# Two ends of an up-projection: a half sum and a copy moved, a whole product ahead of a wait, a bank copied out, and three scan bursts tied

## The chip, the cores and the metric

One core of a Trainium2 chip runs the whole program. The metric is the device time of one execution in microseconds (us), taken as the median of several runs.

## The reference, cut to what matters

The reference is one layer of a diffusion backbone with 128 prompt tokens and 1024 latent tokens (a 16 x 64 grid), model width 1024, all in fp32.

```python
h = rmsnorm(x, norm1) * (1 + scale1) + shift1
mix, new_gla, new_hgrn = hybrid_mixer(h, ...)     # two gated linear scans, forward and backward, then @ w_out
x = x + gate1 * mix
h = rmsnorm(x, norm2) * (1 + scale2) + shift2
u = dw_conv(h @ w_up, conv_w, conv_b, grid)       # 3x3 on the grid; width 3 over the prompt
gate, up = jnp.split(u, 2, axis=-1)               # FFN_HIDDEN = 2816 each
x = x + gate2 * ((jax.nn.silu(gate) * up) @ w_down)
y = rmsnorm(x, final_norm)
```

The scans run in eight heads of two kinds. The change touches the last of the scans and the line `u = dw_conv(h @ w_up ...)`; everything else is as it was.

## The kernel before, in words

**Numbers.** Each fp32 operand of a large product is split into a high half (a rounded fp32r copy, made by ACT) and a low half (the rest, made by DVE or POOL on line 69). PE then computes high x high, high x low and low x high. So a weight tile costs one ACT instruction, one DVE or POOL instruction and three products.

**Order.** A framework places the instructions of each engine: in a simulated schedule it takes, for each engine, what is ready by its model of costs and of priority. `tc.issue_after(ins)` adds an order: what is issued under it comes behind `ins` on its engine. `run(eng, fn)` chains the steps of the first hidden group this way. What carries no such tie can come out in another order than in the text. The names in `anchor` hold the instructions to which later ones are tied.

**Scan stage** (to about 600 us). The loop runs over six head groups `n`, in each over three thirds (`bi`, with block `b` from `ORDER = (2, 1, 0)`), in each over eight slots with two parts. In slots 0, 2, 4 and 6 `levels` issues a burst of small PE products (L964) under high priority. Between the bursts `stream(goal, ...)` issues the fill: products of projections and of w_out that the bursts don't depend on (L625, L639, L777), as far as `GOALS` say for this slot. `anchor["fill"]` is the last fill product and `anchor["paced"]` is the one behind which the next burst is tied. For `n < 5` that tie is set anew in every even slot. The last group, `n == 5`, pops it at its start, so its bursts have none; its fill is the gate weights' L625, evacuated by ACT on L676.

**Up stage** (about 780 to 1270 us). The loop runs over 22 hidden groups `c` of 128 gate and 128 up channels. The product of a group's weights with the 1024 latent tokens is done in seven half-size products instead of eight, as Strassen's method does: `up(c, p)` with p from 1 to 7, each 12 PE instructions of 512 columns (`up_product`, L1777). Their operands are token sums (`b11`, `b21`, `b22`, `t1` to `t4`, made once) and weight sums (`s1` to `s4`, made for each group). They collect in PSUM in two tiles of a group, `F, S = u[c]`; there are three such tiles in all. In between, ACT copies three partial results to SBUF (`copy`, L1971: product 1 to `p1`, product 6 to `u2`, product 5 to `p5`) and DVE adds them: `p1` and `u2` to the halves of F (L2134 and L2135; L1869 and L1870 for the first group), `p5` to S (L2160). Then `conv_rows` forms the 3x3 convolution: ACT's first tap (L1931) and eight DVE steps (L1943) for each half of the channels. `second_gate` applies silu (ACT, L2043), multiplies gate by up on POOL (L2045) and stores it from POOL's queue.

The prompt's product (`up_prompt`, L2009) goes into a bank of its own; it is copied to SBUF and turned by two PE transposes (`prompt_columns`) into a bank `pp` from the same pool `ps_p`. `conv_prompt` reads `pp` with an ACT tap (L1956) and two DVE steps (L1960) for gate and up, four DVE steps in a group.

Weights of the next groups are split with POOL's help: `split_slots` issues ACT's high half (L1759) and POOL's low half (L69); `weight_sums` are POOL's too, and the loads of a row that waits for its tile (`load_row`) stand in SP's queue.

At `c == 21`, the last group, product 3 is issued in two: its first two of four row blocks (`range(2)`, six PE instructions), then the third `u` tile is taken and product 1 issued, then the other six. The third tile comes free when the convolution that reads it has ended.

**Down stage** (from about 1270 us). Seven products (`product`, L2279, L2333), each over eleven pairs of hidden groups, with four row tiles; in the first one the first three pairs go together (`head=3`). `load_w` loads a pair, ACT splits its high half (L133), and the low half (L69) is POOL's for the first pairs and DVE's from then on. The PSUM banks of this stage lie where those of the up stage lay.

Of the kernel before, what the change touches and what calls it, by code (L numbers as in the profile page):

```python
# [12 lines left out]
AF = mybir.ActivationFunctionType  # L13
ALU = mybir.AluOpType
# [3 lines left out]
P = 128  # L18
# [6 lines left out]
NHID = 22  # L25
# [24 lines left out]
def kernel(ctx: ExitStack, tc: tile.TileContext, ins, outs, stop=None):  # L50
    nc = tc.nc
# [10 lines left out]
    anchor = {}  # L62
# [339 lines left out]
    for i in range(2):  # L402
# [3 lines left out]
        for v in range(2):  # L406
            dst = bass.AP(t.tensor, t.offset + v * pitch, [[32 * pitch, 2], [1, 512]])
# [4 lines left out]
    for i in range(2):  # L412
        ps = (ps_a, ps_mm)[i].tile([2 * 32, 512], F32, name="ada", tag=("ada", "mm")[i])
        psA.append(ps)
        for kt in range(KT):
# [4 lines left out]
            for j in range(2):  # L420
# [4 lines left out]
                    start=(kt == 0),  # L425
                    stop=(kt == KT - 1),
# [754 lines left out]
    def ada_load(spare=False):  # L1181
        if ada_todo:
            g, kt, half = ada_todo.pop(0)
            if spare:
                piece = flat(vp.tile([P, NTILE, P], F32, name="v", tag="v"))[:, 0:1024]
                piece = piece.rearrange("p (j n) -> p j n", j=4)
            else:
                piece = rawp.tile([P, 4, 256], F32, name="raw", tag="raw")
            n0 = "ABC".index(g) * 2048
            src = w_ada[kt * P : (kt + 1) * P, n0 : n0 + 2048].rearrange("p (j h n) -> p h j n", j=4, h=2)  # L1190
            nc.sync.dma_start(piece, src[:, half])
            ada_open.append((g, kt, half, piece))
# [41 lines left out]
    for n, u in enumerate(groups):  # L1234
        if not u.gla:
            u.v = [u.vpair[u.hd % 2]]
        if n == 0:
            start_group(u)
            ready = gates(u, 2)
        if n == 5:  # L1240
            anchor.pop("paced")
        for bi, b in enumerate(ORDER):
            fb, k, k0 = ready
            lv = levels(u, b, fb, k, k0)
            for slot in range(8):
                at = 8 * bi + slot
                last = anchor["mm"] = next(lv)
                if (2, 0, 6) <= (n, bi, slot) < (5, 0, 0) and slot % 2 == 0:
                    with tc.issue_after(last.ins):
                        with tc.high_priority(offset=BURST_AHEAD):  # L1250
                            ada_product()
                        ada_load(spare=(n, bi) >= (2, 2))
                with tc.issue_after(last.ins):
                    outs_.step("half", at)
                    states.step("product")
                if slot == 5 and (b > 0 or n < 5):
                    if b > 0:
                        ready = gates(u, b - 1)
                    else:
                        start_group(groups[n + 1])  # L1260
                        ready = gates(groups[n + 1], 2)
                for part in range(2):
                    with tc.issue_after(last.ins):
                        if part == 0:
                            states.step("keys")
                            if n == 5:
                                while slots["held"]:
                                    slots["held"].pop(0)()
                        outs_.step("full", at)
                        if part == 1:  # L1270
                            outs_.step("full", at)
                    goal = GOALS[n] + (GOALS[n + 1] - GOALS[n]) * (16 * bi + 2 * slot + part + 1) / 48
                    stream(goal, None if n == bi == 0 else anchor["mm"] if n == 5 else last)
                    if n < 5 and slot % 2 == 0 and part == 1:
                        anchor["paced"] = anchor["fill"]
            drain(lv)
            states.drain()
            states = Steps(state_steps(u, b, k))
        outs_.drain()
        outs_ = Steps(out_steps(u))  # L1280
# [13 lines left out]
    def run(eng, fn):  # L1294

        if ran.get("free"):
            return fn()
        with tc.issue_after(ran[eng].ins) if eng in ran else nullcontext():
            ran[eng] = fn()
# [103 lines left out]
    tt = nc.vector.tensor_tensor  # L1403
# [7 lines left out]
    def half_hi(nm, n, raw):  # L1411
        run("act", lambda: nc.scalar.activation(HB["h"][nm][:, :, pieces[n]], raw, AF.Copy))
# [255 lines left out]
    p1_t = h2t1.tile([P, 512], F32, name="cp1")  # L1668
# [92 lines left out]
    def split_slots(c, names, eng):  # L1761
        hi, lo = split_parts(c, names)
        hi()
        return lo(eng)
# [5 lines left out]
        eng.tensor_tensor(r["s4"], r["12"], r["s2"], op=ALU.subtract)  # L1770
        return eng.tensor_tensor(r["s3"], r["11"], r["21"], op=ALU.subtract)

    def up_product(dst, c, a, b, start, stop, kts=range(4)):
        n = 3 * kts[0]
        for kt in kts:
            for x, y in (("h", "h"), ("h", "l"), ("l", "h")):
                last = mm(  # L1777
                    dst,
                    w_slot(c, a, x)[:, kt, :],
                    HB[y][b][:, kt, :],  # L1780
                    start=(start and n == 0),
                    stop=(stop and n == 11),
                    skip_group_check=True,
                )
                n += 1
        return last
# [71 lines left out]
    def first_sums():  # L1858

        F, S = u[0]  # L1860
        for n in range(2):
            token_sum(tmp[2 + n], rb(1, 0, n), tmp[2 + n])
        new_tiles("t4", 1)
        run("dve", lambda: tt(S[:, 512:NS], S[:, 0:512], copies["p5"], op=ALU.add))
        half_hi("t4", 0, tmp[2])
        half_hi("t4", 1, tmp[3])
        for n in range(2):
            half_lo("t4", n, tmp[2 + n])
        run("dve", lambda: tt(F[:, 0:512], F[:, 0:512], copies["p1"], op=ALU.add))  # L1869
        run("dve", lambda: tt(F[:, 512:NS], F[:, 512:NS], copies["u2"], op=ALU.add))  # L1870
        second_lo("11", "12", eng="dve")

# [2 lines left out]
    copies = {"u2": u2p5[:, 0], "p5": u2p5[:, 1], "p1": p1_t}  # L1875
# [90 lines left out]
    def chained(fn):  # L1966

        run("pe", fn)
# [4 lines left out]
            return run("act", fn)  # L1973
        anchor["copy"] = fn()

    def up(c, p, kts=range(4)):

        if p in (2, 3, 5):
            Z, Y = u[c][0][:, 0:512], u[c][0][:, 512:NS]
        else:  # L1980
            X = u[c][1][:, 0:512]
        chained(
            {
                1: lambda: up_product(X, c, "11", "b11", True, False),
                2: lambda: up_product(Z, c, "12", "b21", True, True),
                3: lambda: up_product(Y, c, "s4", "b22", False, True, kts),
                4: lambda: up_product(X, c, "22", "t4", False, True),
                5: lambda: up_product(Y, c, "s1", "t1", True, False),
                6: lambda: up_product(X, c, "s2", "t2", False, False),
                7: lambda: up_product(X, c, "s3", "t3", False, False),  # L1990
            }[p]
        )
        if p == 5 and c:
            copy(c, "p5", Y)
        elif p == 1:
            copy(c, "p1", X)
        elif p == 6:
            copy(c, "u2", X)
# [22 lines left out]
    def prompt_columns(c):  # L2021
        pp = ps_p.tile([P, 2, P], F32, name="x", tag="x")

        def turned():
            for i in range(2):
                last = nc.tensor.transpose(pp[:, i, :], pt_t[:, i * P : (i + 1) * P], ident)
            return last

        chained(turned)
        up_first = SLOT[c]["21"] < SLOT[c]["11"]  # L2030
        with after("conv") if c < 2 else nullcontext():
            conv_prompt(pp[:, 1 if up_first else 0, :], c, acc[c][0])
            conv_prompt(pp[:, 0 if up_first else 1, :], 22 + c, acc[c][1])
# [25 lines left out]
    for c in range(NHID + 1):  # L2059
        n = c + 1 if c + 1 < NHID else None  # L2060
# [8 lines left out]
        if c < NHID:  # L2069
            up(c, 5)  # L2070
# [21 lines left out]
        last_c = c == NHID - 1  # L2092
        if c > 0:
            up(c, 2)
            if not last_c:
                up(c, 3)
        pks[c] = ps_p.tile([P, 2 * P], F32, name="x", tag="x")
        if c == 1:
            up_prompt(c, 0)
            up_prompt(c, 1)  # L2100
        if c > 0:
            if last_c:
                up(c, 3, range(2))
            u[c].append(ps_u.tile([P, NS], F32, name="u", tag="u"))
            up(c, 1)
            if c == 1:
                anchor["p1"] = anchor["copy"]
                second_gate(0)
            if last_c:
                up(c, 3, range(2, 4))  # L2110
        if 1 < c and not last_c:
            up_prompt(c, 0)
        up(c, 6)
# [9 lines left out]
        if c and n:  # L2123
            with tc.issue_after(anchor["p1"].ins) if c == 1 else nullcontext():
                split_slots(n, ("s1",), nc.gpsimd)
                split_slots(n, ("11", "12"), nc.gpsimd)
            if n + 1 < NHID:
                load_row(n + 1, 1)
        F, S = u[c]
# [174 lines left out]
    p1, u2, u3 = {}, {}, {}  # L2304
# [127 lines left out]
```

## Time and profile before

| | us |
|---|---|
| median of 3 runs | 1519.78 (1519.69 to 1520.42) |
| the profiled execution | 1517.37 |
| its span in the trace | 1515.2 |
| busy in the span: PE | 1464.7 |
| busy: DVE | 1145.1 |
| busy: ACT | 781.1 |
| busy: POOL | 705.0 |
| DVE's convolution steps (L1943, 352 instructions) | 426.9 |

Times in the trace are counted from the start of the span. A row of the timeline gives start, duration, engine, line, operation, output <- inputs by the program's names, shape, and in brackets the idle time ahead of it with what ended it. A wait in brackets is put down to the release that came last. PE is TensorE's products, PEld its weight loads, DVE VectorE, ACT ScalarE, POOL GpSimd, SP the engine whose queue starts most loads. A row of groups gives least, median and largest duration in nanoseconds behind the count.

### The profile page before, as it was taken

Reading aid. Unit: us, or ns where it says so; the run is one execution under the profiler, and the core shown is the slowest. Engines: PE = TensorE matmul, PEld = TensorE weight load, DVE = VectorE, ACT = ScalarE, POOL = GpSimd, SP = SyncE. Lnnn points to the kernel's source line nnn. Section 1 sums busy time; section 2 is a strip of 40 time slices with the busy share of each in tenths; the row PEclk is TensorE's granted clock in tenths of the full one; section 3 lists DMA queues with packets and bytes.
Section 4 is the critical chain, followed back from the end, with each engine's and each line's share of the span. In section 5 each row is a group of like instructions: output and inputs, shape, how many; then the busy total and the mean of one; then the engine's idle time right before and its main releaser. Section 6 shows DMA issues by size and latency. Waiting matters only on the chain.

```text
span 1515.2 us, 31139 instructions
## 1 busy us (share of the span) xinstructions
PE 1464.7 (97%) x12509; PEld 1247.6 (82%) x12509; DVE 1145.1 (76%) x1735; ACT 781.1 (52%) x1519; POOL 705.0 (47%) x537
## 2 busy tenths in 40 slices
PE   6999999999999999899998999999999999999998
PEld 2898998999898988777776888888888877888886
DVE  3766566565565767755699999999999999689575
ACT  3575667555455455613765444444444444466444
POOL 1602122334333241222229999999999996100001
PEclk9999999999999999999999999999999999999999
DMA  9311111335535463967642745445644567989762
GB/s 341 134 44 48 45 57 52 117 98 171 162 97 184 120 203 121 334 247 251 219 142 89 244 115 144 119 119 139 196 119 139 169 154 215 371 267 368 241 191 115
DMA packets 173802, 253.79 MB, mean 167 GB/s; under 512 B 11828, under 2 KB 113698, under 8 KB 171738
## 3 DMA queue, kind: packets, MB, share of 16 engines
q1 hardware_dynamic: 150455, 173.52, 36.0%
q0 software_dynamic: 22592, 77.60, 16.6%
q8 instruction: 98, 1.61, 0.5%
q10 hardware_dynamic: 611, 0.68, 0.1%
q14 instruction: 46, 0.38, 0.1%
HBM read 191.93 MB, written 82.90 MB: 181 GB/s over the span
## 4 chain that ended last, share of the span: by engine, by line
PE 79%; DVE 7%; DMA 5%; ACT 3%; issue 3%; POOL 2%; SPq 0%; POOLq 0%; DVEq 0%; ACTq 0%
PE u L1777 24%; PE mm L625 15%; PE xb L2279 8%; PE yb L2279 6%; PE mm L639 5%; PE x L2009 4%; PE lv L964 3%; DVE acc L1943 3%; PE mm L777 2%; PE yb L2333 2%; PE u L1544 2%; PE x L1032 1%; PE mm L519 1%; DMA raw<-in_w_in_dram 1%; PE ada L1201 1%
## 5 line engine op out<-in xcount | busy, mean ns | idle before, releaser
L1943 DVE SCALAR_TENSOR_TENSOR acc<-u,convc,acc 128x945 f32<-128x945 f32 (+2 forms) x352 | 426.9, 1218 | 8.9 <-ACT acc L1931 1.8
L69 POOL TENSOR_TENSOR wl<-raw,wh 128x1024 fp32r<-128x1024 f32 x42 | 103.0, 2466 | 249.8 <-ACT wh L133 194.2
L625 PE MATMUL mm<-h1h,wh 128*128 128x384 f32 x528 | 185.0, 350 | 1.3 <-ACT qj L528 1.3
L625 PE MATMUL mm<-h1l,wh 128*128 128x384 f32 x528 | 179.0, 339 | 0.0
L625 PE MATMUL mm<-h1h,wl 128*128 128x384 f32 x528 | 179.0, 339 | 0.0
L927 DVE TENSOR_TENSOR Q<-Q,fb 128x384 f32<-128x384 f32 x126 | 81.9, 650 | 82.4 <-PE lv L964 81.4
L69 POOL TENSOR_TENSOR wul<-sr,wuh 128x512 fp32r<-128x512 f32 (+1 forms) x64 | 115.0, 1799 | 38.6 <-ACT wuh L1759 38.6
L69 POOL TENSOR_TENSOR wul<-ra,wuh 128x1024 fp32r<-128x1024 f32 x43 | 110.0, 2559 | 6.6 <-ACT wuh L133 6.5
L917 ACT ACTIVATE m<-k 128x384 f32<-128x384 f32 x126 | 70.2, 557 | 79.9 <-DVE k L929 37.2
L2243 POOL TENSOR_TENSOR sq<-sq,mhalf 128x1 f32<-128x1 f32 x9 | 11.1, 1231 | 205.8 <-DVE sq L2242 205.8
L625 PEld LDWEIGHTS mm<-h1h,wh 128*128 128x128 f32 x528 | 99.5, 188 | 6.2 <-issue 3.9
L625 PEld LDWEIGHTS mm<-h1l,wh 128*128 128x128 f32 x528 | 99.5, 188 | 0.6 <-issue 0.2
L625 PEld LDWEIGHTS mm<-h1h,wl 128*128 128x128 f32 x528 | 99.3, 188 | 0.8 <-issue 0.5
L639 PE MATMUL mm<-wh,h1h 128*128 128x256 f32 x288 | 83.8, 291 | 1.5 <-ACT v L664 1.5
L929 DVE TENSOR_TENSOR k<-k,fb 128x384 f32<-128x384 f32 x126 | 74.2, 589 | 12.3 <-ACT m L917 7.2
L639 PE MATMUL mm<-wh,h1l 128*128 128x256 f32 x288 | 80.4, 279 | 0.0
L639 PE MATMUL mm<-wl,h1h 128*128 128x256 f32 x288 | 80.4, 279 | 0.0
L133 ACT ACTIVATE wh<-raw 128x1024 fp32r<-128x1024 f32 x50 | 52.8, 1058 | 38.5 <-PE mm L625 11.6
L1971 ACT ACTIVATE u2p<-u 128x512 f32<-128x512 f32 x44 | 26.5, 602 | 77.3 <-PE u L1777 76.7
L1759 ACT ACTIVATE wuh<-ra 128x1024 fp32r<-128x1024 f32 x42 | 44.3, 1054 | 36.6 <-issue 22.1
L2045 POOL TENSOR_TENSOR acc<-acc,acc 128x1152 f32<-128x1152 f32 x22 | 60.0, 2730 | 5.0 <-DVE acc L1943 5.0
L1759 ACT ACTIVATE wuh<-sr 128x512 fp32r<-128x512 f32 (+1 forms) x63 | 48.7, 773 | 23.1 <-PE x L2009 16.4
(385 smaller groups left out, 4464.1 us busy)
## 6 DMA issues: line engine op xcount, KB each, us to landing
ra<-in_w_ffn_up_dram SPq DMA_DIRECT2D x84, 256.0 KB, 3.5
raw<-in_w_in_dram SPq DMA_DIRECT2D x32, 512.0 KB, 4.5
v<-in_w_ada_dram SPq DMA_DIRECT2D x27, 512.0 KB, 5.1
scr_g<-acc POOLq DMA_DIRECT2D x22, 576.0 KB, 5.6
scr_s<-late POOLq DMA_DIRECT2D x11, 1024.0 KB, 4.3
scr_t<-in_w_ffn_down_dram POOLq DMA_DIRECT2D x16, 704.0 KB, 7.3
wa<-in_w_ada_dram SPq DMA_DIRECT2D x16, 512.0 KB, 5.3
scr_t<-in_w_ffn_down_dram POOLq DMA_DIRECT2D x2, 2816.0 KB, 12.5
```

Source lines behind the costliest of these rows:

```text
L69: return eng.tensor_tensor(out, full, hi.bitcast(F32), op=ALU.subtract)
L625: anchor["fill"] = mm(ps, a[:, kt, :], h[kt][b], start=(n == 0), stop=(n == 23))
L639: anchor["fill"] = mm(ps, h[kt][t // 3][:, ts_], a[:, kt % 4, :], start=(n == 0), stop=(n == 23))
L917: nc.scalar.activation(aps(t, 0, [[2 * h, NB], [h, 2], [1, h]]), aps(src, 0, [[2 * h, NB], [BL + h, 2], [1, h]]), AF.Copy)
L927: nc.vector.tensor_tensor(qm, qm, aps(ff_, 2 * h - 1, [[BL - h, 2], [2 * h, NB], [0, h]]), op=ALU.mult)
L929: nc.vector.tensor_tensor(km, km, aps(ff_, BL + 2 * h - 1, [[-(BL + h), 2], [2 * h, NB], [0, h]]), op=ALU.mult)
L1759: return lambda: nc.scalar.activation(hi, raw, AF.Copy), lambda eng: split_lo(eng, lo, raw, hi)
L1777: last = mm(dst, w_slot(c, a, x)[:, kt, :], HB[y][b][:, kt, :], start=(start and n == 0), stop=(stop and n == 11), skip_group_check=True,)
L1943: last = nc.vector.scalar_tensor_tensor(o, u3[:, r0 + dy : r1 + dy, c0 + dx : c1 + dx], wc(3 * (dy + 1) + dx + 1), o, op0=ALU.mult, op1=AL ...
L2009: last = mm(pk, HB[h]["p"][:, 4 * half + kt, :], aps(flat(W[x]), a * 512 + kt * P, [[(b - a) * 512, 2], [1, P]]), start=(half + kt + n == ...
L2045: last = nc.gpsimd.tensor_tensor(accg, accg, accu, op=ALU.mult)
L2279: anchor["down"] = mm(banks[i][:, cs], w[a][:, ts_], w[b][:, 512 + cs.start : 512 + cs.stop], start=(start and j == 0 and n == 0), stop=(j ...
```

## The change

Five edits:

1. **Scan, last group.** The tie of the fourth group's kind goes on into `n == 5`: it is popped at the first and second third (`bi` 0 and 1). In between, in the even slots of the first third, `paced` becomes `lag`, the fill product that was last one even slot earlier. So three bursts of the first third are tied behind the fill of one burst interval back.
2. **First hidden group.** In `first_sums`, the half sum `F[:, 0:512] += p1` (DVE) moves ahead of the two halves of `t4`, in the chain of DVE's steps.
3. **Second group (`c == 1`).** The split of weights `11` and `12` for group 2 is tied behind `anchor["copy"]`, which is now the copy of product 6 (`u2`), instead of behind `anchor["p1"]`.
4. **Last group (`c == 21`), product 3.** It is issued whole, all 12 PE instructions, before the third `u` tile and product 1. The argument `kts` goes.
5. **Last group, prompt.** ACT copies the turned bank `pp` to the first 256 columns of the SBUF tile `p1_t`, which otherwise holds `p1`; `conv_prompt` reads this copy.

```diff
-        if n == 5:
-            anchor.pop("paced")
         for bi, b in enumerate(ORDER):
+            if n == 5 and bi in (0, 1):
+                anchor.pop("paced", None)
...
-                    if n < 5 and slot % 2 == 0 and part == 1:
-                        anchor["paced"] = anchor["fill"]
+                    if slot % 2 == 0 and part == 1:
+                        if n < 5:
+                            anchor["paced"] = anchor["fill"]
+                        elif bi < 1 and "lag" in anchor:
+                            anchor["paced"] = anchor["lag"]
+                        anchor["lag"] = anchor["fill"]
...
-    def up_product(dst, c, a, b, start, stop, kts=range(4)):
-        n = 3 * kts[0]
-        for kt in kts:
+    def up_product(dst, c, a, b, start, stop):
+        n = 0
+        for kt in range(4):
...
         run("dve", lambda: tt(S[:, 512:NS], S[:, 0:512], copies["p5"], op=ALU.add))
+        run("dve", lambda: tt(F[:, 0:512], F[:, 0:512], copies["p1"], op=ALU.add))
         half_hi("t4", 0, tmp[2])
         half_hi("t4", 1, tmp[3])
         for n in range(2):
             half_lo("t4", n, tmp[2 + n])
-        run("dve", lambda: tt(F[:, 0:512], F[:, 0:512], copies["p1"], op=ALU.add))
...
         chained(turned)
+        if c == NHID - 1:
+            held = p1_t[:, 0 : 2 * P]
+            nc.scalar.activation(held, pp.rearrange("p i n -> p (i n)"), AF.Copy)
+            pp = held.rearrange("p (i n) -> p i n", i=2)
...
             up(c, 2)
-            if not last_c:
-                up(c, 3)
+            up(c, 3)
...
-            if last_c:
-                up(c, 3, range(2))
             u[c].append(ps_u.tile([P, NS], F32, name="u", tag="u"))
             up(c, 1)
...
-            if last_c:
-                up(c, 3, range(2, 4))
...
             with tc.issue_after(anchor["p1"].ins) if c == 1 else nullcontext():
                 split_slots(n, ("s1",), nc.gpsimd)
+            with tc.issue_after(anchor["copy"].ins) if c == 1 else nullcontext():
                 split_slots(n, ("11", "12"), nc.gpsimd)
```

More of the change, by code (lines that the diff above doesn't have):

```diff
@@ L1974, in copy, with up @@
         anchor["copy"] = fn()
-    def up(c, p, kts=range(4)):
+    def up(c, p):
         if p in (2, 3, 5):
@@ L1985, in up @@
                 2: lambda: up_product(Z, c, "12", "b21", True, True),
-                3: lambda: up_product(Y, c, "s4", "b22", False, True, kts),
+                3: lambda: up_product(Y, c, "s4", "b22", False, True),
                 4: lambda: up_product(X, c, "22", "t4", False, True),
```

## The prediction

> **What bounds the kernel now.** I read the page first, then stretches of the span, then the timeline of one engine at a time around each edited place.
>
> ```profile
> span 1515.2 us, 31139 instructions
> PE 1464.7 (97%) x12509; PEld 1247.6 (82%) x12509; DVE 1145.1 (76%) x1735; ACT 781.1 (52%) x1519; POOL 705.0 (47%) x537
> 787.00:834.00 47.00, 41.01 (x199) 33.08 (x197) 44.89 (x48) 24.27 (x31) 41.70 (x26) 1.00 0.27 80
> 860.00:1240.00 380.00, 380.00 (x1862) 314.82 (x1861) 369.33 (x390) 177.38 (x237) 365.58 (x244) 1.00 0.53 146
> 1297.00:1477.00 180.00, 180.00 (x796) 149.04 (x795) 127.99 (x140) 100.62 (x116) 3.75 (x1) 1.00 0.83 285
> ```
>
> The last three rows give a stretch, its length, then busy us of PE, PEld, DVE, ACT and POOL. From 860 to 1240 PE never rests, and DVE (369 of 380) and POOL (366) nearly never. From 1297 on only PE is full. So what PE gains or loses before 860, or between 1240 and 1297, should reach the end one to one; only the two ends of the up stage can move the time. A margin of 0.2% is 3.04 us, about what a measurement of this kernel can tell from no change.
>
> **The tie in the scan.** It puts three bursts of head group 5's first third behind the fill one interval back.
>
> ```profile
> 596.05 0.34 PE L625 MATMUL mm<-h1h,wl 128*128 128x384 f32 x1
> 596.42 0.49 ACT L676 ACTIVATE g<-mm 128x384 f32<-128x384 f32 x1 [1.23 <-PE mm L625]
> 596.76 0.40 PE L964 MATMUL lv<-Q,m 128*32 128x32 f32 x24
> 600.69 0.34 PE L625 MATMUL mm<-h1h,wl 128*128 128x384 f32 x1
> 600.96 0.54 PE L964 MATMUL lv<-Q,m 128*32 128x64 f32 x24
> ```
>
> By `GOALS` (28.6 x 27648 columns at the start, 124723 over 48 steps, 384 a product) the gate weights' fill has issued 57 of its products at the end of slot 0 and 84 at the end of slot 2. The product at 596.05 is the 72nd, since ACT evacuates the third block of 24 right behind it; 12 more follow up to 600.69, the 84th, and the last burst comes directly after. So the tightest tie, behind the 84th, is already kept, as are the two looser ones. Cost 0.
>
> **Start of the up stage: the half sum and the copy.** First PE's waits, then DVE and ACT around the edits.
>
> ```profile
> 797.88 0.50 PE L1777 MATMUL u<-b11h,wuh 128*128 128x512 f32 x1 [1.20 <-DVE acc L1943]
> 801.58 0.50 PE L1777 MATMUL u<-t2h,wuh 128*128 128x512 f32 x1 [0.69 <-ACT cp L1971]
> 806.01 0.50 PE L1777 MATMUL u<-t3h,wuh 128*128 128x512 f32 x1 [1.41 <-ACT u2p L1971]
> 809.49 0.47 PE L1777 MATMUL u<-t1h,wuh 128*128 128x512 f32 x1 [0.47 <-DVE acc L1943]
> 834.18 0.47 PE L1777 MATMUL u<-t1h,wuh 128*128 128x512 f32 x1 [2.28 <-DVE acc L1943]
> 782.76 2.36 DVE L69 TENSOR_TENSOR t4l<-acc,t4h 128x1024 fp32r<-128x1024 f32 x2 [0.52 <-ACT t4h L1412]
> 785.04 0.69 DVE L1869 TENSOR_TENSOR u<-u,cp 128x512 f32<-128x512 f32 x1
> 785.77 0.70 DVE L1870 TENSOR_TENSOR u<-u,u2p 128x512 f32<-128x512 f32 x1
> 809.26 0.69 DVE L2160 TENSOR_TENSOR u<-u,u2p 128x512 f32<-128x512 f32 x1
> 828.41 0.70 DVE L2135 TENSOR_TENSOR u<-u,u2p 128x512 f32<-128x512 f32 x1 [0.99 <-ACT u2p L1971]
> 805.38 0.57 ACT L1971 ACTIVATE u2p<-u 128x512 f32<-128x512 f32 x1
> L1943 DVE SCALAR_TENSOR_TENSOR acc<-u,convc,acc x352: 1189/1206/1269, 787.8 to 1281.4; 128x945 f32<-128x945 f32 x88, 128x1008 f32<-128x1008 f32 x44, 128x960 f32<-128x960 f32 x44
> ```
>
> The half sum (L1869, 0.69) moves into the 0.52 that DVE idles before the t4 halves. They come some 0.1 later, which PE's idle 1.20 at 797.88 covers, and everything behind on DVE comes 0.6 sooner: 785.77 - 785.04 = 0.73, less 0.1. The first convolution ends 0.6 sooner, so PE starts at 797.28.
>
> The copy at 805.38 goes ahead of the split that now runs before it on ACT and can start when product 6 ends: 801.58 + 12 x 0.23 + 0.2, near 804.6. PE's 1.41 shrinks by 0.7 and the split, with POOL's half behind it, comes 0.6 later; its weights are wanted only after 809, and the loads in SP's queue that wait for its tile follow 0.6 later into a stretch whose DMA share is 0.27. But PE's next wait (809.49) is on DVE's convolution, which the copy does not speed, so at best both edits give 0.7. And L2160 needs product 7, which would end 1.3 sooner (0.6 + 0.7) against the convolution's 0.6. L2160 stands now where its product has just ended; one convolution step (the L1943 row: median 1.206) earlier it would push the end of the convolution back by its own 0.6 and PE would start where it does now. At 828 DVE waits for PE, so nothing is won there either. Ends: 0 and -0.7. I take -0.1, since the order in the row goes by readiness.
>
> **End of the up stage: whole product, and the bank copied out.**
>
> ```profile
> 1248.14 0.39 PE L1777 MATMUL u<-b22h,wul 128*128 128x512 f32 x1
> 1249.81 0.50 PE L1777 MATMUL u<-b11h,wuh 128*128 128x512 f32 x1 [1.28 <-DVE acc L1943]
> 1271.72 0.47 PE L2279 MATMUL xb<-wuh 128*128 128x512 f32 x1 [2.07 <-DVE acc L1960]
> 1276.15 0.39 PE L2279 MATMUL xb<-wul,wuh 128*128 128x512 f32 x1
> 1289.75 0.39 PE L2279 MATMUL xb<-wul,wuh 128*128 128x512 f32 x1
> 1256.95 0.60 ACT L1971 ACTIVATE u2p<-u 128x512 f32<-128x512 f32 x1 [3.48 <-PE u L1777]
> 1258.39 1.05 ACT L133 ACTIVATE wuh<-ra 128x1024 fp32r<-128x1024 f32 x1
> 1259.31 1.22 DVE L69 TENSOR_TENSOR wl<-ra,wh 128x1024 fp32r<-128x1024 f32 x1
> 1267.06 0.34 DVE L1960 SCALAR_TENSOR_TENSOR acc<-x,convc,acc 128x127 f32<-128x127 f32 x1
> 1271.23 0.34 DVE L1960 SCALAR_TENSOR_TENSOR acc<-x,convc,acc 128x127 f32<-128x127 f32 x1
> 1283.66 3.70 DVE L69 TENSOR_TENSOR wul<-sr,wuh 128x1024 fp32r<-128x1024 f32 x1
> 1259.53 3.27 POOL L69 TENSOR_TENSOR wul<-ra,wuh 128x1024 fp32r<-128x1024 f32 x1 [6.53 <-ACT wuh L133]
> 1265.14 2.68 POOL L2045 TENSOR_TENSOR acc<-acc,acc 128x1152 f32<-128x1152 f32 x1
> 1268.48 5.10 POOL L69 TENSOR_TENSOR wl<-raw,wh 128x1024 fp32r<-128x1024 f32 x2
> 1273.16 2.79 POOL L69 TENSOR_TENSOR wul<-sr,wuh 128x1024 fp32r<-128x1024 f32 x1
> ```
>
> PE issues 60 products from 1276.15 to 1289.75, 0.227 each. Six more ahead of the wait end at 1249.5: the 1.28 goes. But those six hid ACT's copy of product 1 after 1249.81; without them product 6 waits for it, 0.69 as at 801.58. So 6 x 0.23 leave and 1.0 of pause and restart comes: PE and ACT are 0.4 sooner from product 6 on (ends 0 and -0.6).
>
> The copy to SBUF, 128x256, takes ACT at most the 0.60 of its 128x512 copy. The first DVE step that needs the prompts is at 1267.06 now, so with the copy ahead of it the bank is free by 1267.7, and PE wants it at 1271.72 - 2.07 = 1269.65, less 0.4: the 2.07 goes. Next late is POOL: the low half of the fourth weight pair, 1273.16 + 2.79 = 1275.95, is used at 1276.15. POOL works on end to end since 1259.53 (one split of the row of five is not shown), which waits for ACT's split at 1258.39, which stands behind the copy at 1256.95: 0.4 sooner. So in this order PE gains about 0.5, not 2.5.
>
> The price is on DVE. The four prompt steps (L1960) now read two tensors from SBUF, while POOL works without a pause.
>
> ```profile
> L1960 DVE SCALAR_TENSOR_TENSOR acc<-x,convc,acc x88: 339/342/353, 797.7 to 1271.2; 128x127 f32<-128x127 f32 x88
> 200.04 2.37 DVE L1049 SCALAR_TENSOR_TENSOR st<-st,tl 128x128 f32<-128x128 f32 x1
> 199.77 2.49 POOL L69 TENSOR_TENSOR wl<-raw,wh 128x1024 fp32r<-128x1024 f32 x1 [13.52 <-ACT wh L133]
> ```
>
> With one input in PSUM none of 88 took over 0.353. The same operation with both inputs in SBUF, started behind a POOL split, took 2.37 and ended 0.15 after it; and the split at 1283.66 took 3.70 beside POOL. [...]
>
> POOL's ends with everything 0.4 sooner and a step or two let in: 1267.4, 1270.9, 1273.3, 1275.9 (the row of two splits halved). Each step, reached a convolution step behind the one before, ends 0.15 behind the POOL instruction that it meets: +0.2, +2.1, +1.1 and +1.0, DVE +4.4 in all (ends 0 and four times the 2.37, 9.5, less the steps themselves). One more race turns: at 1259.31 DVE's split is 0.2 ahead of POOL's; with POOL 0.4 sooner POOL has it, DVE waits for a whole split of 2.4 to 2.5 and ends 2.0 later (ends 0 and 2.1; the start times of the two rows speak for 2.0). Together DVE +6.4. What hides this is slack: DVE's split of the ninth pair ends at 1283.66 + 3.70 = 1287.36 and is used at 1289.75, 2.4 less a tenth for the signal. PE: 6.4 - 2.3 = +4.1, whatever it had won before.
>
> **Sum.** Scan 0, start -0.1, end +4.1: +4.0. The profiled execution took 1517.37 (2.17 around its span), so 1521.4; the median, 1519.78, is 2.41 above it: **1523.8**.
>
> **Rivals.** (a) POOL does not get ahead at 1259 (the margin is 0.2, and DVE's split may stand a step earlier): DVE +4.4, PE +2.1, 1521.8. For it: the margin. (b) The steps do not wait, because they read past POOL's pauses (its DMA issues) or the rule spares them; POOL keeps its order: start -0.1 to -0.7, end -0.5, 1518.8. Against it: POOL's row of splits without a gap. (c) Faster: as (b), and POOL takes the fourth pair before the two of 1268.48, since ACT's splits come sooner. PE then has its 0.4, the 2.07 and 0.2 of restart, -2.65, cut to -2.3 if DVE's ninth pair stays where it is; with -0.7 at the start -3.0 to -3.35, 1516.6 in the middle. Its far end is the four waits whole, 1.20 + 1.41 + 1.28 + 2.07 = 5.96, less the 1.0 of pause in product 6: -5.0, 1514.8. For it: every edit sits on a PE wait of the rows, 1.20, 1.41, 1.28 and 2.07. Against: the ninth pair's slack. (d) The tie binds after all and holds the first third back: its last two bursts start 4.2 us apart now (596.76, 600.96); at 2 us more for each of three the scan's end, and with it PE, lose up to 6: 1525.8. Against: the rows above.
>
> **How the numbers follow.** Forecast 0.36 (own range 1522.0 to 1525.0, 0.33 of it beyond +3.04), (a) 0.17 (0.03 beyond), (b) 0.11, (c) 0.32 (0.27 beyond -3.04), (d) 0.04. Slower 0.33 + 0.03 + 0.04 = 0.40; faster 0.27; the rest 0.33. The range goes from 1515.6, which leaves out a sixth of (c) near its far end, to the forecast's upper bound and a little of (d), 1525.2.
>
> **What would show it.** Right: no 2.07 at PE's nineteenth down product; L1960 of group 21 over 1 us, ending with POOL's instructions; DVE's last convolution step ending 4 to 6 us later after PE; a PE wait on DVE's split at the eighth or ninth pair. A 0.69 between products 1 and 6 of group 21, the 1.20 near 0.6, the 1.41 near 0.7. Scan bursts in the same order. Wrong: L1960 still at 0.35, or the ninth pair's split no later against PE than now; then (b) or (c).

## The result, and the profile after

The changed kernel takes 1525.16 us (median of 6 runs, 1524.53 to 1526.52); the kernel before took 1519.74 in the same comparison. The ratio is 1.0036 with a 95% interval of 1.0023 to 1.0048: **slower by 5.4 us**, more than the 4.0 forecast. 1525.16 is just inside the range given (to 1525.2); the ratio times the 1519.78 that the prediction started from, 1525.25, is just outside. The profiled execution of the changed kernel is near its median (1525.44); that of the kernel before lay 2.4 below its own, so the two traces differ by 7.8 us and the medians by 5.4.

The page, and PE's waits from 560 to 1300 us at the edited places (sum, times, longest):

```profile
span 1523.0 us, 31143 instructions
PE 1467.7 (96%) x12509; PEld 1250.6 (82%) x12509; DVE 1153.9 (76%) x1735; ACT 780.3 (51%) x1520; POOL 705.0 (46%) x537
PE xb L2283 <- DVE wul L69: 7.2, 1, 7.2
PE u L1781 <- DVE acc L1947: 2.9, 2, 2.0
PE xb L2283 <- POOL wul L69: 1.6, 1, 1.6
PE u L1781 <- ACT cp L1975: 1.4, 2, 0.7
PE u L1781 <- ACT u2p L1975: 1.0, 2, 0.7
```

DVE is 8.8 us busier (1153.9 against 1145.1) with the same number of instructions. The wait on the prompts' bank is gone, and a wait of 7.2 on a DVE split stands where there was none. Lines are four further down than before: L1964 are the prompt steps, L1947 the convolution, L2283 the first down product.

The timeline of PE at the edited places, then of DVE, POOL and ACT at the end of the up stage:

```profile
796.51 0.50 PE L1781 MATMUL u<-b11h,wuh 128*128 128x512 f32 x1 [0.92 <-DVE acc L1947]
803.92 0.50 PE L1781 MATMUL u<-t3h,wuh 128*128 128x512 f32 x1 [0.69 <-ACT u2p L1975]
808.91 0.72 PE L1781 MATMUL u<-t1h,wuh 128*128 128x512 f32 x1 [1.98 <-DVE acc L1947]
832.76 0.39 PE L1781 MATMUL u<-t1h,wuh 128*128 128x512 f32 x1
1274.21 0.50 PE L2283 MATMUL xb<-wul,wuh 128*128 128x512 f32 x1 [1.63 <-POOL wul L69]
1292.60 0.79 PE L2283 MATMUL xb<-wul,wuh 128*128 128x512 f32 x1 [7.22 <-DVE wul L69]
...
1257.52 1.22 DVE L69 TENSOR_TENSOR wl<-ra,wh 128x1024 fp32r<-128x1024 f32 x1
1266.45 2.07 DVE L1964 SCALAR_TENSOR_TENSOR acc<-cp,convc,acc 128x127 f32<-128x127 f32 x1
1266.45 9.72 DVE L1964 SCALAR_TENSOR_TENSOR acc<-cp,convc,acc 128x127 f32<-128x127 f32 x2
1277.28 0.60 DVE L1964 SCALAR_TENSOR_TENSOR acc<-cp,convc,acc 128x127 f32<-128x127 f32 x2
1291.33 1.22 DVE L69 TENSOR_TENSOR wul<-ra,wuh 128x1024 fp32r<-128x1024 f32 x1
...
1258.25 2.76 POOL L69 TENSOR_TENSOR wul<-ra,wuh 128x1024 fp32r<-128x1024 f32 x1 [6.11 <-ACT wuh L133]
1265.71 2.66 POOL L2053 TENSOR_TENSOR acc<-acc,acc 128x1152 f32<-128x1152 f32 x1
1269.04 2.81 POOL L69 TENSOR_TENSOR wl<-raw,wh 128x1024 fp32r<-128x1024 f32 x1
1271.39 2.77 POOL L69 TENSOR_TENSOR wul<-sr,wuh 128x1024 fp32r<-128x1024 f32 x1
1274.33 1.69 POOL L1902 TENSOR_TENSOR late<-acc 128x512 f32<-128x512 f32 x1
...
1265.15 0.37 ACT L2036 ACTIVATE cp<-x 128x256 f32<-128x256 f32 x1
1281.57 1.17 ACT L2051 ACTIVATE acc<-acc 128x1152 f32<-128x1152 f32 x1 [15.13 <-DVE acc L1947]
```

Read the DVE rows against the POOL rows. The first prompt step ends at 1268.52, which is 0.15 after POOL's gate (1265.71 + 2.66 = 1268.37). The next row (x2) holds the first step and the second. The second ends at 1276.17 (1266.45 + 9.72), 7.7 us later: it sat out two whole splits and ended 0.15 after the token sum behind them (1274.33 + 1.69 = 1276.02). By then POOL had nothing more to do, and the last two steps took 0.60 together. So DVE reached the eighth pair's split at 1291.33, not at 1282.53, and PE waited for it. The copy itself is short (ACT, 0.37). ACT's silu of this group waited 15.13 for DVE, and the high halves of the later pairs stood behind it, but they were done well before DVE's low half, which ended PE's wait.

The same PE instructions in the two traces, counted from each span's start. The 0.65 of the first row is not the change's: PE's order is the same up to there, and between 45 and 600 us the difference drifts from +0.8 to −0.5.

| PE instruction | before | after | after − before |
|---|---|---|---|
| group 0, first `t4` product | 784.42 | 783.77 | −0.65 |
| group 1, product 1 | 797.88 | 796.51 | −1.37 |
| group 1, product 7 | 806.01 | 803.92 | −2.09 |
| group 1, product 5 | 809.49 | 808.91 | −0.58 |
| group 2, product 5 | 834.18 | 832.76 | −1.42 |
| down, 1st product | 1265.31 | 1263.93 | −1.38 |
| down, 19th (the bank) | 1271.72 | 1268.11 | −3.61 |
| down, fourth pair's low half | 1276.15 | 1274.21 | −1.94 |
| down, eighth pair's low half | 1287.03 | 1292.60 | +5.57 |
| ten products on | 1289.30 | 1297.03 | +7.73 |

The last step of the table is not a wait but the clock. By stretches (length, PE busy, granted clock, DMA share, GB/s), the changed kernel:

```profile
809.00:812.00 3.00, 3.00 (x8) 0.50 0.53 157
1292.00:1296.00 4.00, 3.40 (x8) 0.50 0.44 131
1296.00:1300.00 4.00, 4.00 (x16) 0.87 0.86 286
```

Behind the waits of 1.98 and of 7.22 us TensorE was granted half its clock for some 3 and 5 us. A product took 0.427 instead of 0.227, which cost 1.6 us at 809 (PE goes from 0.58 ahead to 1.02 behind) and 2.2 at 1293. The first was made good: before, PE waited 2.28 at 834, and after the change it arrives there without a wait.

### The profile page after: what moved, and what is told of

Read it like the earlier page. It is cut to its first block, busy times and chain, and to the rows that moved or that the text cites. A ratio compares the mean times of both kernels' runs of the same rounds, so it can differ in the third digit from the quotient of the medians.

```text
span 1523.0 us, 31143 instructions
## 1 busy us (share of the span) xinstructions
PE 1467.7 (96%) x12509; PEld 1250.6 (82%) x12509; DVE 1153.9 (76%) x1735; ACT 780.3 (51%) x1520; POOL 705.0 (46%) x537
## 4 chain that ended last, share of the span: by engine, by line
PE 78%; DVE 7%; DMA 6%; issue 4%; ACT 3%; POOL 2%; SPq 0%; POOLq 0%; DVEq 0%; ACTq 0%
PE u L1781 24%; PE mm L625 15%; PE xb L2283 7%; PE yb L2283 6%; PE mm L639 5%; PE x L2013 4%; PE lv L964 3%; PE mm L777 2%; DVE acc L1947 2%; PE yb L2337 2%; PE u L1548 2%; PE x L1032 1%; PE mm L519 1%; DMA raw<-in_w_in_dram 1%; DMA wa<-in_w_ada_dram 1%
## 5 line engine op out<-in xcount | busy, mean ns | idle before, releaser
L1947 DVE SCALAR_TENSOR_TENSOR acc<-u,convc,acc 128x945 f32<-128x945 f32 (+2 forms) x352 | 426.9, 1218 | 8.8 <-ACT acc L1935 1.7
L2051 ACT ACTIVATE acc<-acc 128x1152 f32<-128x1152 f32 x22 | 25.7, 1170 | 72.4 <-DVE acc L1947 72.4
```

The costliest lines, as they stand in the source:

```text
L1947: last = nc.vector.scalar_tensor_tensor(o, u3[:, r0 + dy : r1 + dy, c0 + dx : c1 + dx], wc(3 * (dy + 1) + dx + 1), o, op0=ALU.mult, op1=AL ...
```

## The experiments

The ratios below are to the kernel before, run on the same chip; 0.1% is 1.5 us. The leading theory ("lock") puts the loss on the prompt steps' second SBUF input; the rivals are the other edits ("rest") and the copy's place in ACT's queue ("ACT").

**One part out, one part in.** From the changed kernel, without the copy:

```diff
-            held = p1_t[:, 0 : 2 * P]
-            nc.scalar.activation(held, pp.rearrange("p i n -> p (i n)"), AF.Copy)
-            pp = held.rearrange("p (i n) -> p i n", i=2)
```

> The changed kernel without the bank copy (group 21's prompt steps read PSUM again); the other four edits stay. Theory 'lock' (the loss is the copy's: two of the four prompt steps, now with both inputs in SBUF, stood 2.07 and 7.73 us behind POOL, and PE waited 7.2 us for the eighth pair's DVE split): L1960's steps of group 21 back at 0.34, the 2.07 wait of PE on the bank back, no wait on a DVE split, time 0.8 us below before (the start of the up stage 0.4 and the whole product 0.4), 1518.9. Rival 'rest' (the other edits lose, by the half clock behind PE's 1.98 us wait at 808.9 and by POOL's new order at the start of the up stage): 2 us or more above before, 1522 or more.

Measured: 1517.5, ratio 0.9984 (0.9976 to 0.9993). PE's waits from 1240 on are 2.1 on the bank and 0.7 on the copy of product 1, nothing else. The other four edits together make the kernel faster, by 0.16%; that is 2.4 us where 0.8 was expected.

The same lines put into the kernel before, alone:

> The kernel before with the bank copy alone. 'Lock': at least one prompt step of group 21 over 2 us and ending with a POOL instruction, DVE's last convolution step 4 to 9 us later, a PE wait on a DVE split of the eighth or ninth pair; POOL stands 0.4 later against DVE than in the changed kernel, so which instructions the steps meet may differ: time 3 to 8 us above before, 1526 in the middle. 'Rest': within 1 us of before. Rival 'ACT' (the copy holds ACT up and with it the splits of the later pairs, the steps' operands don't matter): slower too, but the steps at 0.34 us.

Measured: 1528.07, ratio 1.0061 (1.0047 to 1.0075). PE's waits from 1240 on, then one prompt step with the first and last of the POOL rows that it met:

```profile
PE xb L2283 <- DVE wul L69: 4.3, 1, 4.3
PE xb L2283 <- POOL wul L69: 2.1, 1, 2.1
PE u L1777 <- DVE acc L1943: 1.3, 1, 1.3
1271.36 8.87 DVE L1960 SCALAR_TENSOR_TENSOR acc<-cp,convc,acc 128x127 f32<-128x127 f32 x1
1270.78 5.15 POOL L69 TENSOR_TENSOR wl<-raw,wh 128x1024 fp32r<-128x1024 f32 x2
1278.41 1.66 POOL L1898 TENSOR_TENSOR late<-acc 128x512 f32<-128x512 f32 x1
```

One step alone took 8.87, through three splits and the sum (1278.41 + 1.66 = 1280.07; it ended at 1280.23). So the copy alone, without the other edits, brings more than the whole loss of the change. The two edits of the start, and the whole product, each alone:

> The kernel before with the two edits of the start of the up stage alone (half sum sooner; second group's split behind the copy of product 6). 'Lock': 0.4 below before, from 0 to 0.8; PE's waits before products 1, 6 and 7 of the second group as in the changed kernel (0.9, 0.7, 0.7), the one before product 5 near 2.0, with products at half clock behind it that a later wait absorbs. 'Rest': 2 us or more above before.

> The kernel before with product 3 of the last group whole ahead of product 1, alone. 'Lock': 0.4 below before: no 1.28 wait ahead of product 1, a wait of 0.69 on the copy of product 1 instead, PE 0.4 sooner at the first down product; POOL's low half of a pair now stands ahead of the second gate. 'Rest': above before, since POOL's new order delays the gate of group 20.

Measured: 1517.56, ratio 0.9989 (0.9977 to 1.0001), and 1518.7, ratio 0.9994 (0.9985 to 1.0004). Each alone is at the limit of what can be told from no change, and both point down. The waits came as expected. The half clock expected behind the wait before product 5 did not come in the first one's trace: the granted clock was 1.00 from 809 to 813, and PE gained 2.1 us between the start of the up stage and 1246, where 0.4 was expected.

**Copy or operand?** The copy is made, and the steps go on reading PSUM:

```diff
             nc.scalar.activation(held, pp.rearrange("p i n -> p (i n)"), AF.Copy)
-            pp = held.rearrange("p (i n) -> p i n", i=2)
```

> The changed kernel with the bank copy made, but the prompt steps still reading PSUM, so the copy is made for nothing. 'Lock' (the operands of the prompt steps): all four steps at 0.34 us, PE's 2.07 wait on the bank back, no wait on DVE's eighth pair, time as without the copy, 1517.5 to 1518.5. Rival 'ACT' (the copy stands in ACT's way): a wait of PE of several us on a split in the down stage, time above 1522.

Measured: 1517.83, ratio 0.9984 (0.9974 to 0.9995), as without the copy. The four steps of group 21 (least, median and largest in ns):

```profile
L1964 DVE SCALAR_TENSOR_TENSOR acc<-x,convc,acc x4: 341/342/351, 1267.9 to 1272.2; 128x127 f32<-128x127 f32 x4
```

ACT made the copy here too (1267.19, 0.38 us). So "ACT" falls: the operand is what costs. Next, POOL taken away: `nc.gpsimd if p == 1 and j < 6 else nc.vector` becomes `nc.vector`.

> The changed kernel with the low halves of the first product's six early pairs on DVE instead of POOL (six splits of 1.22, 7.3 us more for DVE, and POOL nearly idle from 1258 on but for the gate of group 20 and a token sum). 'Lock': the second prompt step no longer 7.7 us; at most one step meets the gate (up to 2.7) and one the sum (up to 1.7), the others 0.34; DVE's convolution ends about when it does in the changed kernel (7.3 more work, some 7 less waiting), time within 3 us of the changed kernel. If the steps were slow for another reason than POOL (the SBUF operand itself, the tile), they stay at 2 and 7.7 and the time goes up by 7.

Measured: 1526.81, ratio 1.0042 (1.0026 to 1.0058). All four steps, still with two SBUF inputs, took 0.33 to 0.34:

```profile
1275.78 0.34 DVE L1964 SCALAR_TENSOR_TENSOR acc<-cp,convc,acc 128x127 f32<-128x127 f32 x1
1277.15 0.60 DVE L1964 SCALAR_TENSOR_TENSOR acc<-cp,convc,acc 128x127 f32<-128x127 f32 x2
1278.85 0.33 DVE L1964 SCALAR_TENSOR_TENSOR acc<-cp,convc,acc 128x127 f32<-128x127 f32 x1
```

POOL stood idle from 1272.5 on, so two SBUF inputs alone cost nothing. Nor did they gain anything: 0.33 to 0.34 here, 0.34 from PSUM. DVE paid in work what it saved in waiting (PE's wait on its split: 7.0 instead of 7.2).

**How long does such a step wait?** The kernel before, with the bank copied back into `pt_t` in each of the groups 2 to 21:

```diff
+        if c > 1:
+            held = pt_t
+            nc.scalar.activation(held, pp.rearrange("p i n -> p (i n)"), AF.Copy)
+            pp = held.rearrange("p (i n) -> p i n", i=2)
```

> The kernel before with the bank copied to SBUF in each of the last twenty groups, so that 80 prompt steps read two SBUF inputs beside a busy POOL. 'One instruction' (as the prediction had it: a step waits for the POOL instruction that it meets): no step over 2.9 us, most between 0.34 and 2.8, DVE 60 to 100 us busier and the time up by about as much. 'Pause' (the step waits until POOL has nothing ready to go on with): steps of 5 us and more, ending 0.15 behind a POOL instruction after which POOL stood idle; the time up by 100 us or more.

Measured: 1736.81, ratio 1.1426, which is 217 us slower for 80 instructions of 0.34 us. The steps' own time makes up 182 of it (209.4 instead of 27). The group of them from 780 on (busy us, mean ns), and one that took longest with the first POOL instruction that it met and the two at its end:

```profile
L1960 DVE SCALAR_TENSOR_TENSOR acc<-late,convc,acc 128x127 f32<-128x127 f32 x80 | 209.4, 2654 | 0.3 <-ACT acc L1956 0.3
1036.85 10.13 DVE L1960 SCALAR_TENSOR_TENSOR acc<-late,convc,acc 128x127 f32<-128x127 f32 x1
1036.06 1.67 POOL L69 TENSOR_TENSOR wul<-sr,wuh 128x512 fp32r<-128x512 f32 x1
1045.22 1.60 POOL L1897 TENSOR_TENSOR late<-late,acc 128x512 f32<-128x512 f32 x1
1046.90 1.26 POOL L1899 TENSOR_TENSOR late<-acc,late 128x512 f32<-128x512 f32 x1
```

The distribution settles it: 43 of the 80 took under 0.5 us, 19 over 5, the longest 10.1. It ended at 1046.98, 0.16 after an instruction of POOL (1045.22 + 1.60) whose successor, which needs its result, started 0.08 after that end. The POOL instructions that it let pass before had a successor that started ahead of their end: over all 36 steps above 1 us in this trace there are 79 such places between computing instructions, each overlapping by 0.03 to 0.5 us. Of the 36, 27 got in where nothing overlapped, four where the overlap was only 0.03, and five behind a DMA issue whose record overlapped. These steps did not wait for the POOL instruction that they met: 27 times of 36 **they waited until POOL's row broke**. Why some DMA issues let a step in and others, such as the one at 1038.54 (0.97 us), did not stays open.

**The clock.** The changed kernel with a filler, 24 unused products put into PE's 7.2 us wait ahead of the eighth pair, first into one free bank, then into another:

```diff
+                junk = ps_d[0].tile([P, 512], F32, name="yb", tag="yb")    # then ps_d[2]
+                for k in range(24):
+                    ...  mm(junk, w[0][:, 0:P], w[0][:, 512:1024], start=(k == 0), stop=(k == 23))
```

> [...] 'Clock' (the half-speed products behind the wait come from the wait itself): granted clock near 1.0 from 1290 to 1300, the ten products behind the wait at 0.227 and not 0.427, time 2 us below the changed kernel, 1523. Otherwise (they are slow for their operands or the loads): clock and time as in the changed kernel, or later by what the filler adds.

> The filler again, in the bank of the half of group 21 whose convolution ends first (near 1280), so that it can start where PE's wait starts. 'Clock': 24 products of 0.227 fill 5.4 of the 7.2 us; the real products behind it run at 0.227 at once, granted clock 1.0 from 1285 to 1300, time 2 us below the changed kernel, 1523. If the clock does not hang on PE's idle time, ten products at 0.427 remain behind the wait and the time is that of the changed kernel.

Measured: 1528.62, ratio 1.0057 (1.0040 to 1.0073), and 1524.91, ratio 1.0031 (1.0020 to 1.0043). The first bank was itself held by DVE's convolution until 1290, so the filler came behind a wait of 4.88 and only added work; but the two together show what the clock hung on here. First kernel, then second, 1285 to 1300:

```profile
1285.00:1290.00 5.00, 0.41 (x2) 0.79 0.07 27
1290.00:1295.00 5.00, 4.72 (x12) 0.53 0.35 107
1295.00:1300.00 5.00, 5.00 (x24) 1.00 0.90 296
...
1285.00:1290.00 5.00, 5.00 (x24) 1.00 0.18 66
1290.00:1295.00 5.00, 4.07 (x18) 1.00 0.32 105
1295.00:1300.00 5.00, 5.00 (x22) 1.00 0.89 296
```

In the first the filler itself ran at half clock and the real products behind it at full; in the second nothing ran at half clock. So the slow products followed PE's idle time (4.88 us ahead of the filler in the first, none there in the second), whatever they were. In time the second kernel was not told apart from the changed kernel: the expected 2 us are not shown by the medians. Its trace shows both the 2 us and where part of them went. From the eighth pair's low half ten products took 2.40 us instead of 4.43, and then PE waited for the ninth pair's split, which the half clock had hidden:

```profile
1294.91 0.50 PE L2292 MATMUL xb<-wul,wuh 128*128 128x512 f32 x1 [0.60 <-DVE wul L69]
```

**What the bank was worth.** Without the copy, and with the third and fourth bank exchanged:

```diff
+    xb[2], xb[3] = xb[3], xb[2]
```

> The changed kernel without the bank copy, and with the third and fourth bank of the first down product exchanged, so that the prompts' bank is wanted nine products (2.04 us) later. 'Lock' (nothing but the operands was wrong with the copy): no wait at the nineteenth product, all prompt steps at 0.34; then POOL's low half of the fourth pair is late, a wait of 1.5, so 0.5 us below the kernel without the copy, 1517.2. If the 2.07 wait had another holder than the bank it stays.

Measured: 1516.43, ratio 0.9973 (0.9963 to 0.9982), but the wait of 2.1 at the nineteenth product is still there, since the edit exchanged only names: the framework gives tiles their banks in the order of their use, so the nineteenth product still went into the prompts' bank, and the program that ran is the one of the first experiment. So it tells nothing about the bank, but the two ratios, 0.9984 and 0.9973, are two measurements of one program. On top of it, POOL's order changed (`tc.issue_after` of the fourth pair's low half for the fifth's and sixth's), and then the seventh pair's low half given to POOL:

> As the bank order, and POOL's low halves of the fifth and sixth pair tied behind the fourth's. No wait on POOL at the fourth pair; PE 2.07 us sooner there than without the copy. Then DVE is next: the eighth pair's split 0.4 late and the ninth's (blocked by POOL's gate of group 21, 3.7) 1.3 late. So 0.8 below the kernel without the copy, 1516.9.

> As the one with the fourth pair first, and the seventh pair's low half on POOL (behind the sixth's) instead of DVE, whose whole chain of group 21 then comes 1.2 us sooner: eighth pair in time, ninth at most 0.3 late. 1.8 below the kernel without the copy, 1516.0, and 0.2 to 0.3% below before. If POOL's row of splits blocks more of DVE's two-input instructions instead, no better than the one before.

Measured: 1517.49 (0.9983, 0.9974 to 0.9992) and 1517.14 (0.9981, 0.9972 to 0.9991). These two have the same line, so the bank's wait remained in both (2.1 and 2.0), and neither tells what was asked. What does free the bank is the order of the prompt's own steps, both ACT taps first and the DVE steps two by two:

```diff
+                for part in ((True, ()), (False, (-1,)), (False, (1,))):
+                    for side in sides:
+                        conv_prompt(*side, *part)
```

> The changed kernel without the bank copy; the prompt steps of group 21 read PSUM, but both ACT taps come first and the four DVE steps follow two by two with one convolution step between, so the bank is free some 2 us sooner without a second SBUF input. Steps at 0.34; PE's 2.07 wait at the nineteenth product down to 0.2 or less. If the prediction's step on POOL holds (its low half of the fourth pair is next late), PE then waits 1.4 to 1.6 at the fourth pair and the time is only 0.5 below the kernel without the copy (1516.4 to 1517.8 in three builds); if it does not hold, 2 below.

> As before it, with POOL's fourth pair ahead of the fifth and sixth and the seventh pair's low half on POOL. No wait on the bank, none on POOL at the fourth pair, at most 0.3 on DVE at the eighth or ninth: 1.8 to 2.0 us below the kernel without the copy, about 1515, 0.3% below before. If DVE's ninth split is next late by more, 0.5 to 1 below.

Measured: 1514.94 (0.9969, 0.9956 to 0.9981) and 1514.95 (0.9969, 0.9955 to 0.9983): both are faster than the kernel before and than the changed one. PE's waits from 1240 on, in the first and in the second:

```profile
PE xb L2287 <- POOL wul L69: 0.8, 1, 0.8
PE u L1781 <- ACT cp L1976: 0.7, 1, 0.7
PE xb L2287 <- DVE acc L1965: 0.6, 1, 0.6
...
PE u L1784 <- ACT cp L1979: 0.7, 1, 0.7
PE xb L2290 <- DVE acc L1968: 0.2, 1, 0.2
```

In the first the bank's wait fell from 2.1 to 0.6 and POOL's fourth pair came late by 0.8. Against the kernel without the copy PE gained 0.5 from the start of the up stage's third group to the fourth pair; with POOL's order mended as well, 1.9. The medians do not tell these two apart, nor do they tell the order of the steps from the kernel without the copy: the intervals of 0.9969 and of 0.9984 and 0.9973 overlap.

## Why the prediction was right or wrong

**The scan.** Right: PE's instructions come in the same order in both kernels, but for product 3. The tie cost 0: the traces differ by −0.47 at 587 and by −0.45 at 607.

**The start.** Right in its steps: product 1 of group 1 gained 0.72 (0.6 said), the wait ahead of it fell only to 0.92, since PE came to it 0.4 sooner as well; the wait on the copy fell from 1.41 to 0.69, L2160 (now L2164) slipped a convolution step ahead, to 806.97, and PE's next wait grew to 1.98, so the gain of 1.44 was gone again at 809.49 (−0.58 against −0.65 at the entry). Wrong in its end: "at 828 DVE waits for PE, so nothing is won there either" missed that PE's own 2.28 wait at 834 goes. In the changed kernel's trace that paid for the half clock behind the 1.98 and left PE 0.77 ahead at 834 and 0.25 at 1246; what took the rest is open. With the start edits alone, where the clock stayed full, it left 2.1, three times the bound of 0.7. So the −0.1 came near by a cost that was not in it.

**The whole product.** The 1.28 went, the 0.69 came; alone it gave a ratio of 0.9994. In the trace of the changed kernel PE stands 0.4 better from product 6 on than just ahead of the edit (−1.28 against −0.90). Right.

**The bank.** The 2.07 went. POOL's fourth pair was next late, as said: a wait of 1.63. The trace of the experiment with the steps in pairs gave 0.5 for the freed bank as long as POOL kept its order, the number of the prediction.

**DVE's price.** The kind of wait was right, the rule for its length was not; this is the step that failed. "Each step ... ends 0.15 behind the POOL instruction that it meets" gave +0.2, +2.1, +1.1 and +1.0, together +4.4. Measured, less the steps themselves: +1.7, +7.4, 0 and 0, together +9.1. The first step waited longer than the +0.2 because POOL's order changed, which the prediction did not expect: a split (1263.36) had moved ahead of the gate, which so ended at 1268.37 and not at 1267.4. The second step is the rule's failure: it did not end behind the split that it met. The row at 200.04, from which the rule was taken, met a POOL instruction that stood alone; those at 1265 stood in a row, and the row had to break. Even the far bound (four times the 2.37, less the steps, 8.1) was passed, because it too was built from single POOL instructions. The race at 1259 was not lost: DVE's split started at 1257.52, POOL's at 1258.25, so the +2.0 for it was nothing; this was the condition of rival (a). So +6.4 became +9.1 on DVE, and its split of the eighth pair came 8.8 later than before. The place (DVE's split of a late pair) holds, but the wait came at the eighth pair, whose slack was 3.3 (1287.03 − 1283.75): PE +5.57 there. At the ninth pair, with the 2.4 of slack that the prediction named, the same delay is worth +6.4 instead of the +4.1 in its sum.

**What was not in the sum.** The half clock behind the 7.22 wait, another 2.2. It hid a wait of some 0.8 at the ninth pair: DVE's split of it ended at 1296.13, and at 0.227 a product PE would have come to it at 1295.3. So it added some 1.3 to the +6.4, which gives the +7.7 of the table.

By the traces the kernel lost 7.8 where +4.0 was said. The medians lie closer, 5.4 apart: the profiled execution of the kernel before lay below its median, and it had more of the clock than most. Over the 95 executions of that kernel that the experiments recorded, the mean granted clock ran from 0.990 to 0.998. The 25 executions with 0.992 or less took 1521.6 on average, the 18 with 0.996 or more 1516.9; the profiled one, at 1517.37, had 0.996. One place where the clock can differ is the wait of 2.28 at 834. In the profiled execution full clock followed it; in the traces with the copy alone and with the whole product alone, which have the same wait, 0.72 and 0.60 followed for the three us behind it. The prediction added the whole 2.41 between profiled execution and median to the changed kernel too, whose profiled execution lay at its median. That wrong step made up for part of what its sum lacked, so that 1523.8 came within 1.4 of the measured time is partly luck.

What the runs show of the contention is this: beside an idle POOL the four steps with two SBUF inputs took 0.33 to 0.34; beside a busy one the step at 1036.85 took 10.13 and sat out seven more instructions of POOL's queue, one of them a DMA issue, than the one that it met. Of the clock they show this: it was 0.53 from 1290 to 1295 with the wait of 4.88, 0.60 from 1295 to 1300 behind the wait of 7.0 (POOL quiet), and 0.50 from 1292 to 1296 behind the 7.22. At the start of the kernel, behind 4.71 before and 4.56 after, it was 1.00 for the three us that followed. Shorter waits went both ways: in the kernel before, 0.50 for three us behind 2.42 at 35.45 and 1.00 behind 2.28 at 834; and over 800 to 815, where PE waits 2.0 ahead of group 1's product 5, 0.89 in the kernels with the bank order and with the fourth pair first, 1.00 in those with the seventh pair on POOL and with the second filler. What decides between the two was not shown.

## What to carry to other kernels

Before an operand moves from PSUM to SBUF, look at what POOL does at that moment: here a 0.34 us DVE step with two SBUF inputs stood up to 10.1 us behind a whole row of POOL instructions, and its price was to be read from where POOL's row next broke, not from the length of one instruction. If a bank is to come free sooner, first try the order of its readers: here that took PE's wait on the bank from 2.1 to 0.6 with no new operand, and with the other four edits the kernel came out 0.31% faster than before. And price a new PE wait with the slow products behind it: with the waits of 4.88, 7.0 and 7.22 us at the end of the up stage they came, at a granted clock of 0.53, 0.60 and 0.50.

## What the runs showed of the hardware

- In the trace with the copy in every group, 27 of the 36 waits above 1 us of a DVE step with two SBUF inputs ended where POOL's next instruction started after the former's end; in the longest, of 10.13 us, a gap of 0.08 us between two dependent POOL instructions was enough. Five ended behind a DMA issue in POOL's queue; in the changed kernel the second step stood through the one of 0.99 us at 1273.69.
- Behind the DMA issue of 1.10 us at 1268.32 in the changed kernel POOL's two 128x1024 splits took 2.81 and 2.77 instead of the 2.41 and 2.39 of the two just ahead of the gate, and their records overlap the next one by 0.46 and 0.47; in the kernel before three behind such an issue, of 1.08 us, took 2.75 to 2.79. The second DVE step found no gap there.
- In the changed kernel half clock (0.50) cost 0.2 us per 512-column product (0.427 against 0.227), for 3.4 us behind the wait of 1.98 and 4.5 us behind that of 7.22.
